# MLP of a hybrid encoder layer on one core: the first quarter of the hidden width takes the schedule of the next two

## The chip, the cores and the metric

One core of one Trainium2 chip runs the whole program as one launch. The metric is the device time of a run in microseconds (us). Three runs of the kernel before are given, and one execution was profiled.

## The reference, cut to what matters

One layer for 256 tokens of width 2048, all in float32: a mixer, a cross-attention, an MLP and a final norm. The change lies in the MLP and at the seam in front of it.

```python
    for l in range(DEPTH):
        ...
        x = x + cross_attention(h, mem_n, w_xq[l], w_xkv[l], w_xo[l])
        h = rms_norm(x, norm_ffn_g[l])
        x = x + jnp.square(jax.nn.relu(h @ w_ff1[l])) @ w_ff2[l]
    return rms_norm(x, norm_final_g)
```

`w_ff1` is 2048 x 8192, `w_ff2` is 8192 x 2048.

## The kernel before

**Precision.** Every matrix is split into a rounded part and the rest ("hi" and "lo", tiles `whi`/`wlo` for weights, the two halves of a `q` tile for activations). A product of two split matrices takes three matmuls, hi by hi, hi by lo and lo by hi. The weights come as float32 from memory, 1 MB a transfer, into one of three `raw` buffers. ScalarE writes hi (L125), VectorE writes lo (L126), in halves of 128x1024 each. There are three buffers for hi and three for lo, and from the MLP on every fourth half goes to a fourth pair, `whx`/`wlx` (`half_tiles`, L79), whose memory is free only once the attention's tiles have been read for the last time.

**The MLP.** The hidden width is worked in four quarters (`for fb in range(4)`, L1382). A quarter has two parts:

- First projection: eight blocks of 256 hidden features (`blocks`, L192 to L222). A block loads 2 MB of `w_ff1` and uses it in four pieces, each eight pairs of matmuls on TensorE (L210: 128x512, then 128x256). Its end is read by ScalarE and VectorE (L219, L220), squared after the ReLU (`evac_h`) and split again. I call the blocks of the first quarter A to H. In the order below, A writes `s_13017`/`s_13018`.
- Second projection: 512 hidden rows by 512 output columns is one block product per half of the tokens. `plain(n, q)` (L1232) computes one such block for both halves of the tokens, 24 matmuls of 128x512. Eight block products (two by two by two) can be had with seven products of sums of blocks (Strassen's form): `product` (L1254) is one of the seven, 12 matmuls; the sums of the weights are made by VectorE in place (L1261) between the products that need them, the sums of activations in `token_sums` (L1188). The four weight blocks of a unit lie in `b11`, `b12`, `b22`, `b21`, which are the tiles `rt` and `tr`, loaded by `load_block` (L1206, 1 MB each).

Quarters 1 to 3 compute two units in seven products. Their generator `with_seven` begins during the first projection, after the blocks D to H (`next(parts_of)`), and their matmuls are chained in one order (`ends`). The first quarter (the `else` branch, L1364 on) computes one unit with seven products and the rest plainly, all behind its first projection, and its matmuls are free to be put in another order by the scheduler.

**The residual.** The attention leaves the residual feature-major in `rt`. Four VectorE transposes (L1124) turn it into `tr`, and `place(b8)` (L1126) copies it from there token-major into `res`: 8 calls of 4 transfers, 64 KB each, in runs of 128 bytes. `tr` and `rt` are free for weight blocks when this is done. Before the transposes a TensorE product with ones (L1042) gives the norm's sums, and VectorE reads them (L1044).

**What sets the order.** Each engine works its instructions in the order in which the scheduler put them at build time. All transfers here are issued by one queue, SP's.

Of the kernel before, what the change touches and what calls it, by code (L numbers as in the profile page):

```python
# [52 lines left out]
def trunk(ctx: ExitStack, tc: tile.TileContext, x_f, mem_f, positions, lead_f, small_f, w_in, ret_gn_g, w_out, w_xq,  # L53
# [96 lines left out]
    def quad_a():  # L150
        return new_quad(hqp, 5)
# [1043 lines left out]
        vec.tensor_sub(sv[:, 3], a12, sv[:, 1])  # L1195
        split([a[:, i, :] for a in s_hl], sv.rearrange("p a s -> p (a s)"))

    def with_seven(hid, rows, last, early):

# [76 lines left out]
            own[n] = ps  # L1276
            opened.difference_update((n, t) for t in range(NT))

        if early:
            load_block(b11, 0, 0)  # L1280
            yield
            load_block(b12, 0, 1)
            product(shared, part(0, 0), b11, "shared", (b11, b12, b11))
            read((0, 0, shared))
            yield
            load_block(b22, 1, 1)
            product(p5, summed(0), b11, "p5", (b11, b22, b11))
            read((1, 0, p5), (1, 1, p5))
            yield
            load_block(b21, 1, 0)  # L1290
            product(shared, summed(1), b11, "shared", (b12, b22, b12))
            read((1, 0, shared))
            yield
            product(shared, summed(2), b12, "shared", (b11, b21, b11))
            read((0, 1, shared), (1, 1, shared))
            if last:
                product(p5, summed(3), b22, "p3")
                read((1, 0, p5))
            yield
            for n in range(2):  # L1300
                take(n, stream_ps())
            plain(0, 2)
            load_block(b12, 0, 3)
            if last:
                final.append(quad_a().both.rearrange("p k s -> p (k s)").bitcast(F32))
                with tc.issue_after(fetched[-1]):
                    nc.sync.dma_start(final[0], norm_final_g.partition_broadcast(P))
            if not last:
                product(own[1][0], summed(3), b22, (1, 0))
            plain(0, 3)  # L1310
            load_block(b22, 1, 3)
            product(own[0][0], part(1, 0), b21, (0, 0))
            read((0, 0, own[0][0], True))
            product(own[0][1], part(1, 1), b11, (0, 1))
            read((0, 1, own[0][1], True))
            plain(1, 2)
            load_block(b11, 0, 2)
            take(2, [bank(), bank()])
            plain(2, 2)
            load_block(b21, 1, 2)  # L1320
            opened.difference_update(("shared", "p5"))
            product(shared, part(0, 0), b11, "shared", (b11, b12, b11))
            read((2, 0, shared))
            plain(1, 3)
            read(*((1, t, own[1][t], True) for t in range(NT)))
            product(p5, summed(0), b11, "p5", (b11, b22, b11))
            read((3, 0, p5), (3, 1, p5))
            plain(2, 3)
            take(3, stream_ps())
            product(own[3][0], summed(3), b22, (3, 0), (b12, b22, b12))  # L1330
            plain(3, 2)
            product(shared, summed(1), b11, "shared", (b11, b21, b11))
            read((3, 0, shared))
            if not last:
                plain(3, 3)
                read(*((3, t, own[3][t]) for t in range(NT)))
                product(own[2][0], part(1, 0), b21, (2, 0))
                read((2, 0, own[2][0]))
                product(shared, summed(2), b12, "shared")
                read((2, 1, shared), (3, 1, shared))  # L1340
                product(own[2][1], part(1, 1), b11, (2, 1))
                read((2, 1, own[2][1]))
            else:
                product(own[2][0], part(1, 0), b21, (2, 0))
                read((2, 0, own[2][0], True), (2, 1, own[2][1]))
                plain(3, 3, True)
                of_7 = parted(b12)
                with tc.issue_after(latest["lo"]), tc.issue_after(latest["hi"]):
                    add(3, 0, own[3][0])
                    of_4 = parted(b11, quad_b)  # L1350
                with tc.high_priority(offset=50000):
                    settle(3, 0)
                    latest["lo"] = latest["add"]
                    mean_square(0)
                    r_0 = factor(0)
                    finish(0, r_0, (0, 512, act, nc.sync), (1024, 1536, act, nc.sync))
                for those in unscaled:
                    scale(*those)
                read((3, 1, own[3][1]))
                product(shared, summed(2), None, "shared", halves=of_7)  # L1360
                read((3, 1, shared, True), (2, 1, shared))
                ends_of = stream_ps()
                product(ends_of, part(1, 1), None, "end", halves=of_4)
                with tc.high_priority(offset=50000):  # L1364
                    with tc.issue_after(latest["square"]):
                        finish(0, r_0, (512, 1024, act, nc.sync), (1536, D, act, nc.sync))
                    junk = fp.tile([P, 2, S], F32, name="hs", tag="hs", bufs=2)
                    for c, ps in enumerate(ends_of):
                        with tc.issue_after(latest["lo"]):
                            got = add(2, 1, ps[:, :256], c * 256, c * 256 + 256)  # L1370
                        acc = ssq4[:, 1, 3 + c:4 + c]
                        vec.scalar_tensor_tensor(junk[:, c], got, 1.0, got, op0=ALU.mult, op1=ALU.mult, accum_out=acc)
                        if c:
                            vec.scalar_tensor_tensor(sums[1], acc, 1.0 / D, sums[1], op0=ALU.mult, op1=ALU.add)
                        else:
                            mean_square(1)
                    finish(1, factor(1), (0, 256, act, nc.sync), (512, 1024, vec, act), (256, 512, act, nc.sync),
                           (1024, 1536, vec, nc.sync), (1536, D, vec, act))
        else:
            for n in range(2):  # L1380
                take(n, stream_ps())
            own[2] = own[3] = [bank(), bank()]  # L1382
            plain(3, 0)
            load_block(b11, 0, 0)
            plain(3, 1)
            load_block(b12, 0, 1)
            product(shared, part(0, 0), b11, "shared", (b11, b12, b11))
            read((0, 0, shared))
            plain(3, 2)
            load_block(b22, 1, 1)  # L1390
            product(p5, summed(0), b11, "p5", (b11, b22, b11))
            read((1, 0, p5), (1, 1, p5))
            plain(0, 2)
            product(own[1][0], summed(3), b22, (1, 0), (b12, b22, b12))
            plain(3, 3)
            load_block(b21, 1, 0)
            read(*((3, t, own[3][t]) for t in range(NT)))
            product(shared, summed(1), b11, "shared", (b11, b21, b11))
            read((1, 0, shared))
            plain(0, 3)  # L1400
            product(own[0][0], part(1, 0), b21, (0, 0))
            read((0, 0, own[0][0]))
            plain(2, 0)
            plain(1, 2)
            product(shared, summed(2), b12, "shared")
            read((0, 1, shared), (1, 1, shared))
            plain(2, 1)
            product(own[0][1], part(1, 1), b11, (0, 1))
            read((0, 1, own[0][1]))
            plain(2, 2)  # L1410
            plain(2, 3)
            read(*((2, t, own[2][t]) for t in range(NT)))
            plain(1, 3)
# [5 lines left out]
    for fb in range(4):  # L1419
        hid = []  # L1420
        rows = w_ff2[0, fb * D:(fb + 1) * D, :]
        early = fb > 0
        parts_of = with_seven(hid, rows, fb == 3, early)
        ends.clear()
        for b2 in range(8):
            hs = fp.tile([P, 2, S], F32, name="hs", tag="hs", bufs=2)
# [1 line left out]
                hid.append(quad_a())  # L1428

            def evac_h(b, ps):  # L1430
                if early:
                    act.activation(ps, ps, AF.Relu)
                    act.activation(hs[:, b, :], ps, AF.Square)
                else:
# [12 lines left out]
        for _ in parts_of:  # L1447
            pass

# [41 lines left out]
```

## Time and profile before

| | |
|---|---|
| runs | 2045.98 us median of 3 (2044.49 to 2046.55) |
| span of the profiled execution, first to last instruction | 2043.3 us |
| the profiled execution's own time | not given apart; the median of the runs is 2.7 us above its span |
| busy share of the span | TensorE 99%, weight loads 86%, VectorE 76%, ScalarE 58%, GpSimd 2% |
| granted TensorE clock, mean | 0.998 |
| moved by DMA | 405.24 MB, mean 198 GB/s |

The busy shares are means over all stages; what a stage is worth has to be read from the stage itself. A busy TensorE is one with a matmul in flight. The pace of the matmuls is read from the distance of their starts, which is less than the duration of one since they overlap.

### The profile page before, as it was taken

How to read it: one execution, taken by the hardware profiler on the slowest of the kernel's cores; microseconds unless marked ns; L12 is line 12 of the kernel's file. 1: busy time of each engine (PE TensorE's matmuls, PEld its weight loads, DVE VectorE, ACT ScalarE, POOL GpSimd, SP SyncE). 2: the span in 40 equal slices, each digit the busy share in tenths (PEclk: the TensorE clock that was granted, in tenths of full speed). 3: DMA queues.
4: the chain of work that ended last, by engine and by line, in shares of the span. 5: the costliest groups of instructions: out<-in, count | busy, mean ns of one | idle time of the engine just before them, and what ended most of it. 6: DMA issues, size and time to landing. Idle time of an engine off the chain costs nothing.

```text
span 2043.3 us, 28453 instructions
## 1 busy us (share of the span) xinstructions
PE 2030.5 (99%) x10802; PEld 1751.4 (86%) x10802; DVE 1550.6 (76%) x2423; ACT 1184.3 (58%) x1941; POOL 38.7 (2%) x50
## 2 busy tenths in 40 slices
PE   9999999999999999999999999999999999999998
PEld 7888888988888888888888899888888888888886
DVE  5887788779667875888567666777867887888788
ACT  6655764575457554755446565555547656656655
POOL 0000000000000000000000000000000000000000
PEclk9999999999999999999999999999999999999999
DMA  9689556466555655555467655569657656665761
GB/s 329 209 259 303 184 185 197 154 189 201 180 166 183 198 190 165 186 181 190 156 212 244 191 183 163 174 180 254 221 168 234 219 163 214 201 204 166 242 231 62
DMA packets 329370, 405.24 MB, mean 198 GB/s; under 512 B 34944, under 2 KB 239632, under 8 KB 329104
## 3 DMA queue, kind: packets, MB, share of 16 engines
q1 hardware_dynamic: 328800, 402.74, 62.2%
q8 instruction: 84, 1.38, 0.3%
q10 hardware_dynamic: 432, 0.69, 0.1%
q14 instruction: 54, 0.44, 0.1%
HBM read 389.74 MB, written 11.55 MB: 196 GB/s over the span
## 4 chain that ended last, share of the span: by engine, by line
PE 97%; DVE 2%; issue 0%; DMA 0%; ACT 0%; SPq 0%; DVEq 0%; POOLq 0%; POOL 0%; ACTq 0%
PE s L210 52%; PE s L167 8%; PE s L168 8%; PE s L166 8%; PE b L1227 7%; PE s L1227 7%; PE s L400 1%; PE s L401 1%; PE s L402 1%; PE b L795 1%; PE b L698 1%; PE b L138 1%; PE b L828 1%; PE b L137 1%; PE b L139 1%
## 5 line engine op out<-in xcount | busy, mean ns | idle before, releaser
L210 PE MATMUL s<-q,whi 128*128 128x512 f32 x2816 | 969.0, 390 | 0.6 <-DVE bo L220 0.6
L126 DVE TENSOR_TENSOR wlo<-raw,whi 128x1024 fp32r<-128x1024 f32 x586 | 715.1, 1222 | 296.3 <-ACT whi L125 291.7
L125 ACT ACTIVATE whi<-raw 128x1024 fp32r<-128x1024 f32 x586 | 620.8, 1060 | 488.9 <-PE s L210 209.2
L210 PE MATMUL s<-q,wlo 128*128 128x256 f32 x2816 | 765.0, 281 | 0.0
L210 PEld LDWEIGHTS s<-q,whi 128*128 128x128 f32 x2816 | 520.6, 188 | 101.4 <-DVE bo L220 0.9
L210 PEld LDWEIGHTS s<-q,wlo 128*128 128x128 f32 x2816 | 527.2, 188 | 12.6 <-DVE wlo L126 0.5
L167 PE MATMUL s<-wlo,q 128*128 128x512 f32 x704 | 277.2, 394 | 0.0
L168 PE MATMUL s<-whi,q 128*128 128x512 f32 x704 | 274.9, 391 | 0.0
L166 PE MATMUL s<-whi,q 128*128 128x512 f32 x704 | 254.4, 391 | 0.0
L166 PEld LDWEIGHTS s<-whi,q 128*128 128x128 f32 x704 | 132.1, 188 | 27.4
L168 PEld LDWEIGHTS s<-whi,q 128*128 128x128 f32 x704 | 132.3, 188 | 26.2
L167 PEld LDWEIGHTS s<-wlo,q 128*128 128x128 f32 x704 | 132.3, 188 | 26.2
L219 ACT ACTIVATE bo<-s 128x256 f32<-128x256 f32 x192 | 73.2, 381 | 105.5 <-PE s L210 105.5
L220 DVE TENSOR_TENSOR bo<-bo,s 128x256 f32<-128x256 f32 x192 | 79.9, 416 | 43.0 <-ACT bo L219 42.8
L1227 PE MATMUL s<-whi,q 128*128 128x512 f32 x280 | 90.4, 389 | 0.0
L1250 DVE TENSOR_TENSOR wlo<-rt,whi 128x1024 fp32r<-128x1024 f32 x54 | 65.8, 1224 | 32.3 <-ACT whi L1249 31.6
L210 PE MATMUL s<-q,whx 128*128 128x512 f32 x256 | 89.2, 389 | 0.0
L125 ACT ACTIVATE whx<-raw 128x1024 fp32r<-128x1024 f32 x58 | 61.5, 1060 | 43.2 <-PE b L1227 17.2
L126 DVE TENSOR_TENSOR wlx<-raw,whx 128x1024 fp32r<-128x1024 f32 x58 | 70.9, 1222 | 17.9 <-ACT whx L125 17.4
L1249 ACT ACTIVATE whi<-rt 128x1024 fp32r<-128x1024 f32 x54 | 57.2, 1060 | 38.1 <-PE s L1227 17.8
L210 PE MATMUL s<-q,wlx 128*128 128x256 f32 x256 | 70.4, 280 | 0.0
L1227 PE MATMUL b<-whi,q 128*128 128x512 f32 x216 | 70.3, 389 | 0.0
(350 smaller groups left out, 2372.2 us busy)
## 6 DMA issues: line engine op xcount, KB each, us to landing
raw<-w_in SPq DMA_DIRECT2D x143, 1024.0 KB
raw<-w_ff SPq DMA_DIRECT2D x100, 1024.0 KB
raw<-w_xkv SPq DMA_DIRECT2D x29, 1024.0 KB
raw<-w_out SPq DMA_DIRECT2D x16, 1024.0 KB
raw<-w_xq SPq DMA_DIRECT2D x16, 1024.0 KB
raw<-w_xo SPq DMA_DIRECT2D x16, 1024.0 KB
rt<-w_ff SPq DMA_DIRECT2D x14, 1024.0 KB
tr<-w_ff SPq DMA_DIRECT2D x14, 1024.0 KB
```

Source lines behind the costliest of these rows:

```text
L125: latest["hi"] = act.activation(hi[:, cs], src[:, cs], AF.Copy).ins
L126: latest["lo"] = vec.tensor_sub(lo[:, cs], src[:, cs], hi[:, cs].bitcast(F32)).ins
L137: pe.matmul(o, lhs[0], rhs[0], start=first, stop=False)
L166: pe.matmul(o, xh, wh, start=first, stop=False)
L167: pe.matmul(o, xh, wl, start=False, stop=False)
L168: pe.matmul(o, xl, wh, start=False, stop=last)
L210: ins = pe.matmul(ps[b][:, :S] if part else ps[b], halves[h][part][:, i, b * P:(b + 1) * P], x[:, kk % 4, :], start=kk == 0 and not part, ...
L219: act.activation(o, ps[b][:, S:], AF.Copy)
L220: vec.tensor_add(o, o, ps[b][:, :S])
L1227: ins = pe.matmul(o, lhs[l], rhs[r], start=key not in opened, stop=last and j == 2, skip_group_check=True).ins
L1249: latest["hi"] = act.activation(hi, raw[:, c:c + 1024], AF.Copy).ins
L1250: latest["lo"] = vec.tensor_sub(lo, raw[:, c:c + 1024], hi.bitcast(F32)).ins
```

## The change

The `else` branch of `with_seven` is gone. The first quarter runs the same code as quarters 1 and 2: two units in seven products, the generator begun after block D, ReLU and square by ScalarE instead of one VectorE instruction, the matmuls of the projection chained in `ends`. So that `rt` and `tr` are free in time, the calls of `place` move forward: one to two after each of the blocks A to F instead of one after each of A to H.

```diff
-    def with_seven(hid, rows, last, early):
+    def with_seven(hid, rows, last):
...
-        if early:
...
-        else:
-            for n in range(2):
-                take(n, stream_ps())
-            own[2] = own[3] = [bank(), bank()]
-            plain(3, 0)
-            load_block(b11, 0, 0)
-            plain(3, 1)
-            load_block(b12, 0, 1)
-            product(shared, part(0, 0), b11, "shared", (b11, b12, b11))
-            read((0, 0, shared))
-            plain(3, 2)
...
-            plain(2, 2)
-            plain(2, 3)
-            read(*((2, t, own[2][t]) for t in range(NT)))
-            plain(1, 3)
-            read(*((1, t, own[1][t]) for t in range(NT)))
...
             def evac_h(b, ps):
-                if early:
-                    act.activation(ps, ps, AF.Relu)
-                    act.activation(hs[:, b, :], ps, AF.Square)
-                else:
-                    vec.scalar_tensor_tensor(hs[:, b, :], ps, 0.0, ps, op0=ALU.max, op1=ALU.mult)
+                act.activation(ps, ps, AF.Relu)
+                act.activation(hs[:, b, :], ps, AF.Square)
...
-            blocks(h3, w_ff1[0], fb * D + b2 * 256, 2, evac_h, ends if early else None)
-            if early and b2 > 2:
+            blocks(h3, w_ff1[0], fb * D + b2 * 256, 2, evac_h, ends)
+            if fb == 0:
+                for b8 in ((0,), (1, 2), (3,), (4, 5), (6,), (7,), (), ())[b2]:
+                    place(b8)
+            if b2 > 2:
                 next(parts_of)
-            if fb == 0:
-                place(b2)
```

What this does to the order of the instructions is shown at three places. Quarters 1 to 3 keep their order on all engines; only the names of the fourth pair of weight buffers fall on other halves.

First, TensorE at the seam, from the end of block A's third piece. Before:

```order
L210 MATMUL s_13018<-q,whi 128x512
L210 MATMUL s_13018<-q,wlo 128x256
L210 MATMUL s_13127<-q,whi 128x512
L210 MATMUL s_13127<-q,wlo 128x256
L210 MATMUL s_13128<-q,whi 128x512
L210 MATMUL s_13128<-q,wlo 128x256
L210 MATMUL s_13127<-q,whi 128x512
L210 MATMUL s_13127<-q,wlo 128x256
L1042 MATMUL b<-ones,acc_12125 128x2 x2
L210 MATMUL s_13128<-q,whi 128x512
```

Here `s_13127` and `s_13128` are block B. Before, B's pieces go on behind these rows, with the first two `whx` matmuls of block A in their midst. After the change, from the same point:

```order
L210 MATMUL s_13018<-q,whi 128x512
L210 MATMUL s_13018<-q,wlo 128x256
L1042 MATMUL b<-ones,acc_12125 128x2 x2
L210 MATMUL s_13017<-q,whx 128x512
L210 MATMUL s_13018<-q,whx 128x512
L210 MATMUL s_13017<-q,wlx 128x256
L210 MATMUL s_13018<-q,wlx 128x256
```

The product with ones moves forward by three pairs, and block A's last piece (`whx`, `wlx`) follows at once. Block B begins only behind it.

Second, VectorE at the same place. Before:

```order
L126 TENSOR_TENSOR wlo<-raw,whi 128x1024 x2
L1044 TENSOR_SCALAR n_s<-b 128x2
L1124 STREAM_TRANSPOSE tr<-rt 128x1024 x4
L126 TENSOR_TENSOR wlx<-raw,whx 128x1024
L1115 TENSOR_TENSOR rstd3q<-n_r 128x2
L126 TENSOR_TENSOR wlo<-raw,whi 128x1024 x2
```

After:

```order
L126 TENSOR_TENSOR wlo<-raw,whi 128x1024
L1044 TENSOR_SCALAR n_s<-b 128x2
L1124 STREAM_TRANSPOSE tr<-rt 128x1024 x4
L126 TENSOR_TENSOR wlo<-raw,whi 128x1024
L1115 TENSOR_TENSOR rstd3q<-n_r 128x2
L126 TENSOR_TENSOR wlx<-raw,whx 128x1024
```

The lo of block B's third piece, before the transposes until now, stands behind them, and ahead of `wlx`, the lo of block A's last piece.

Third, SP's queue from the fifth load of `w_ff1` on (`raw`: half of a block's weights, 1 MB; `res`: a transfer of `place`; `rt`, `tr`: `load_block`). Before:

```order
L113 DMA raw<-w_ff 128x8x256 x5
L1131 DMA res<-tr 32x16x32 x2
L113 DMA raw<-w_ff 128x8x256
L1131 DMA res<-tr 32x16x32 x3
L113 DMA raw<-w_ff 128x8x256
L1131 DMA res<-tr 32x16x32 x4
L113 DMA raw<-w_ff 128x8x256
L1131 DMA res<-tr 32x16x32 x7
L113 DMA raw<-w_ff 128x8x256 x2
L1131 DMA res<-tr 32x16x32 x4
```

After:

```order
L113 DMA raw<-w_ff 128x8x256 x5
L1131 DMA res<-tr 32x16x32 x4
L113 DMA raw<-w_ff 128x8x256
L1131 DMA res<-tr 32x16x32 x10
L113 DMA raw<-w_ff 128x8x256
L1131 DMA res<-tr 32x16x32 x2
L113 DMA raw<-w_ff 128x8x256
L1210 DMA rt<-w_ff 128x4x512
L1131 DMA res<-tr 32x16x32 x7
L113 DMA raw<-w_ff 128x8x256
L1131 DMA res<-tr 32x16x32
L113 DMA raw<-w_ff 128x8x256
```

Ahead of the first load of block E (the ninth `raw`) stand 23 transfers of `place` and one weight block, where there were 16 transfers of `place`.

## Rows read from the trace of the kernel before

**Rows 1.** The page, part 1: busy time, share of the span, instructions.

```profile
PE 2030.5 (99%) x10802; PEld 1751.4 (86%) x10802; DVE 1550.6 (76%) x2423; ACT 1184.3 (58%) x1941; POOL 38.7 (2%) x50
```

**Rows 2.** TensorE's waits: for whom, us in total, times, longest.

```profile
PE s L210 <- DVE bo L220: 0.6, 1, 0.6
```

**Rows 3.** Stretches: us, busy us (instructions) by engine, clock, DMA share, GB/s.

```profile
1335.00:1340.00 5.00, 5.00 (x31) 4.45 (x30) 3.73 (x6) 2.88 (x6) 0.00 (x0) 1.00 0.62 193
1368.00:1457.00 89.00, 88.42 (x485) 76.60 (x483) 67.13 (x106) 47.29 (x70) 0.00 (x0) 1.00 0.96 267
1425.00:1430.00 5.00, 5.00 (x31) 4.38 (x30) 3.55 (x6) 2.62 (x5) 0.00 (x0) 1.00 1.05 392
1540.00:1700.00 160.00, 160.00 (x816) 136.78 (x815) 131.98 (x153) 96.97 (x133) 0.00 (x0) 1.00 0.60 196
```

**Rows 4.** Timeline of TensorE, second projection: start, us, engine, line, operation.

```profile
1460.17 0.62 PE L1227 MATMUL s<-whi,q 128*128 128x512 f32 x2
...
1462.89 0.39 PE L1227 MATMUL s<-whx,q 128*128 128x512 f32 x1
```

**Rows 5.** Timeline of TensorE at the seam; in brackets idle time and releaser.

```profile
1357.14 0.39 PE L210 MATMUL s<-q,whi 128*128 128x512 f32 x1
...
1357.48 0.50 PE L1042 MATMUL b<-ones,acc 128*128 128x2 f32 x4
1357.84 0.47 PE L210 MATMUL s<-q,whi 128*128 128x512 f32 x1
...
1362.38 0.63 PE L210 MATMUL s<-q,whx 128*128 128x512 f32 x2
...
1367.93 0.28 PE L210 MATMUL s<-q,wlx 128*128 128x256 f32 x1
1368.79 0.50 PE L210 MATMUL s<-q,whi 128*128 128x512 f32 x1 [0.58 <-DVE bo L220]
```

**Rows 6.** Timeline of VectorE at the seam.

```profile
1355.19 1.23 DVE L126 TENSOR_TENSOR wlo<-raw,whi 128x1024 fp32r<-128x1024 f32 x1 [1.08 <-ACT whi L125]
...
1358.82 0.15 DVE L1044 TENSOR_SCALAR n_s<-b 128x2 f32<-128x2 f32 x1
1358.88 4.61 DVE L1124 STREAM_TRANSPOSE tr<-rt 128x1024 f32<-128x1024 f32 x4
1363.42 1.18 DVE L126 TENSOR_TENSOR wlx<-raw,whx 128x1024 fp32r<-128x1024 f32 x1
1364.52 0.15 DVE L1115 TENSOR_TENSOR rstd3q<-n_r 128x2 f32<-128x2 f32 x1
1364.59 2.35 DVE L126 TENSOR_TENSOR wlo<-raw,whi 128x1024 fp32r<-128x1024 f32 x2
1368.31 0.42 DVE L220 TENSOR_TENSOR bo<-bo,s 128x256 f32<-128x256 f32 x1 [1.37 <-ACT bo L219]
```

**Rows 7.** Timeline of ScalarE: at the seam, and block E's first load.

```profile
1356.58 1.06 ACT L125 ACTIVATE whi<-raw 128x1024 fp32r<-128x1024 f32 x1 [1.43 <-PE s L210]
1358.02 1.06 ACT L125 ACTIVATE whx<-raw 128x1024 fp32r<-128x1024 f32 x1 [0.38 <-PE b L1042]
...
1391.75 1.06 ACT L125 ACTIVATE whi<-raw 128x1024 fp32r<-128x1024 f32 x1 [4.14 <-DMA raw<-w_ff]
```

**Rows 8.** The clock behind the last matmuls: a stretch, columns as in rows 3.

```profile
2034.00:2036.00 2.00, 0.00 (x0) 0.00 (x0) 1.72 (x7) 1.86 (x4) 0.00 (x0) 0.82 0.49 182
```

**Rows 9.** Timeline of TensorE: its last matmuls.

```profile
2030.30 3.03 PE L1227 MATMUL s<-q 128*128 128x256 f32 x24
```

**Rows 10.** Timeline of SP's queue: issues of transfers.

```profile
1386.32 7.05 SPq L1131 DMA_DIRECT2D res<-tr  x4
...
1414.56 6.90 SPq L1131 DMA_DIRECT2D res<-tr  x4
```

**Rows 11.** The page, part 5: the lo of weights on VectorE; mean ns behind the busy time.

```profile
L126 DVE TENSOR_TENSOR wlo<-raw,whi 128x1024 fp32r<-128x1024 f32 x586 | 715.1, 1222 | 296.3 <-ACT whi L125 291.7
```

**Rows 12.** Line L1261 on VectorE, sums of weight blocks: duration in ns, min/median/max.

```profile
L1261 DVE TENSOR_TENSOR rt<-tr,rt x42: 1215/1218/1220, 1454.9 to 2015.9; 128x1024 f32<-128x1024 f32 x42
```

More of the change, by code (lines that the diff above doesn't have):

```diff
@@ new lines, in with_seven @@
+        load_block(b11, 0, 0)
+        yield
+        load_block(b12, 0, 1)
+        product(shared, part(0, 0), b11, "shared", (b11, b12, b11))
+        read((0, 0, shared))
+        yield
+        load_block(b22, 1, 1)
+        product(p5, summed(0), b11, "p5", (b11, b22, b11))
+        read((1, 0, p5), (1, 1, p5))
+        yield
+        load_block(b21, 1, 0)
+        product(shared, summed(1), b11, "shared", (b12, b22, b12))
+        read((1, 0, shared))
+        yield
+        product(shared, summed(2), b12, "shared", (b11, b21, b11))
@@ new lines, in with_seven @@
+        read((0, 1, shared), (1, 1, shared))
+        if last:
+            product(p5, summed(3), b22, "p3")
+            read((1, 0, p5))
+        yield
+        for n in range(2):
+            take(n, stream_ps())
+        plain(0, 2)
+        load_block(b12, 0, 3)
+        if last:
+            final.append(quad_a().both.rearrange("p k s -> p (k s)").bitcast(F32))
+            with tc.issue_after(fetched[-1]):
+                nc.sync.dma_start(final[0], norm_final_g.partition_broadcast(P))
@@ new lines, in with_seven @@
+        if not last:
+            product(own[1][0], summed(3), b22, (1, 0))
+        plain(0, 3)
+        load_block(b22, 1, 3)
+        product(own[0][0], part(1, 0), b21, (0, 0))
+        read((0, 0, own[0][0], True))
+        product(own[0][1], part(1, 1), b11, (0, 1))
+        read((0, 1, own[0][1], True))
+        plain(1, 2)
+        load_block(b11, 0, 2)
+        take(2, [bank(), bank()])
+        plain(2, 2)
+        load_block(b21, 1, 2)
+        opened.difference_update(("shared", "p5"))
@@ new lines, in with_seven @@
+        product(shared, part(0, 0), b11, "shared", (b11, b12, b11))
+        read((2, 0, shared))
+        plain(1, 3)
+        read(*((1, t, own[1][t], True) for t in range(NT)))
+        product(p5, summed(0), b11, "p5", (b11, b22, b11))
+        read((3, 0, p5), (3, 1, p5))
+        plain(2, 3)
+        take(3, stream_ps())
+        product(own[3][0], summed(3), b22, (3, 0), (b12, b22, b12))
+        plain(3, 2)
+        product(shared, summed(1), b11, "shared", (b11, b21, b11))
+        read((3, 0, shared))
@@ new lines, in with_seven @@
+        if not last:
+            plain(3, 3)
+            read(*((3, t, own[3][t]) for t in range(NT)))
+            product(own[2][0], part(1, 0), b21, (2, 0))
+            read((2, 0, own[2][0]))
+            product(shared, summed(2), b12, "shared")
+            read((2, 1, shared), (3, 1, shared))
+            product(own[2][1], part(1, 1), b11, (2, 1))
+            read((2, 1, own[2][1]))
+        else:
+            product(own[2][0], part(1, 0), b21, (2, 0))
+            read((2, 0, own[2][0], True), (2, 1, own[2][1]))
+            plain(3, 3, True)
+            of_7 = parted(b12)
+            with tc.issue_after(latest["lo"]), tc.issue_after(latest["hi"]):
+                add(3, 0, own[3][0])
+                of_4 = parted(b11, quad_b)
+            with tc.high_priority(offset=50000):
+                settle(3, 0)
+                latest["lo"] = latest["add"]
+                mean_square(0)
+                r_0 = factor(0)
+                finish(0, r_0, (0, 512, act, nc.sync), (1024, 1536, act, nc.sync))
+            for those in unscaled:
+                scale(*those)
+            read((3, 1, own[3][1]))
+            product(shared, summed(2), None, "shared", halves=of_7)
+            read((3, 1, shared, True), (2, 1, shared))
+            ends_of = stream_ps()
+            product(ends_of, part(1, 1), None, "end", halves=of_4)
+            with tc.high_priority(offset=50000):
+                with tc.issue_after(latest["square"]):
+                    finish(0, r_0, (512, 1024, act, nc.sync), (1536, D, act, nc.sync))
+                junk = fp.tile([P, 2, S], F32, name="hs", tag="hs", bufs=2)
+                for c, ps in enumerate(ends_of):
+                    with tc.issue_after(latest["lo"]):
+                        got = add(2, 1, ps[:, :256], c * 256, c * 256 + 256)
+                    acc = ssq4[:, 1, 3 + c:4 + c]
+                    vec.scalar_tensor_tensor(junk[:, c], got, 1.0, got, op0=ALU.mult, op1=ALU.mult, accum_out=acc)
+                    if c:
+                        vec.scalar_tensor_tensor(sums[1], acc, 1.0 / D, sums[1], op0=ALU.mult, op1=ALU.add)
+                    else:
+                        mean_square(1)
+                finish(1, factor(1), (0, 256, act, nc.sync), (512, 1024, vec, act), (256, 512, act, nc.sync),
+                       (1024, 1536, vec, nc.sync), (1536, D, vec, act))
@@ L1421, in trunk @@
         rows = w_ff2[0, fb * D:(fb + 1) * D, :]
-        early = fb > 0
-        parts_of = with_seven(hid, rows, fb == 3, early)
+        parts_of = with_seven(hid, rows, fb == 3)
         ends.clear()
```

118 lines of the change are left out of this document (removed).

## The prediction

> **What bounds the kernel now.** I read the page's busy times first [rows 1]: TensorE is busy in 99% of the span, so a change pays only if TensorE gets fewer matmuls or has fewer gaps. Then TensorE's waits [rows 2]: in the whole MLP it waits once, 0.6 us, at the seam between the attention's last projection and the first quarter [rows 5]. In a stretch of quarter 1, which has the schedule that the first quarter is to get, it is busy in 160 of 160 us at full clock, with VectorE at 132 and ScalarE at 97 [rows 3]. So the matmuls that go are worth their pace, and a new gap costs its length. The rest is read at the seam, from the timelines of TensorE, VectorE and ScalarE [rows 5 to 7], and for the transfers from the stretches [rows 3] and SP's queue [rows 10].
>
> **The matmuls that go.** Before, the first quarter has 12 plain blocks of 24 matmuls and 7 products of 12: 372. After, 8 and 14: 360. Twelve matmuls started between 1460.17 and 1462.89 [rows 4], 2.72 us or 0.227 each (the 0.39 in the row is a duration, and they overlap). The twelve that go are worth **2.72 us**.
>
> **What VectorE and ScalarE get.** Two more products than plain blocks taken out, at two halves each: 3 x 2 = 6 more splits (14 products and 8 plain blocks are 22 units of 1 MB, against 19), 1.22 us each on VectorE [rows 11]; 8 more sums of weight blocks at 1.22 [rows 12]; six more adds into the residual; against that, 16 ReLU instructions leave for ScalarE. The splits and sums are 14 x 1.22 = 17 us more on VectorE, and the adds and the ReLUs about balance. I cost it at nothing: quarter 1 carries the same load, and TensorE doesn't wait there [rows 3]. Without that cover, each late half would cost up to 1.22.
>
> **The seam.** Here the change moves two things, and a chain that was hidden comes to light. Before, TensorE did the product with ones at 1357.48, worked on with block B, came to A's last piece (`whx`) at 1362.38 only and to `wlx` after that [rows 5]. In that shelter VectorE read the norm's sums at 1358.82, transposed for 4.54 us (start to next start) and wrote `wlx` from 1363.42 [rows 6]. After, A's last piece follows the product with ones at once, and `wlx` stands behind the transposes and one more half. In steps:
>
> - Three pairs at 0.34 (1357.14 to 1357.48) now stand behind the product with ones instead of ahead: it starts at 1356.46. It takes TensorE 0.36 (to 1357.84), until 1356.82. Its result released ScalarE 0.54 after its start (1358.02 [rows 7]), so it is there at 1357.00.
> - ScalarE writes block B's third hi from 1356.58 for 1.06 [rows 7], then `whx`, until 1358.70. TensorE follows a release by 0.06 (VectorE's read of 1368.31 ends at 1368.73, TensorE starts at 1368.79 [rows 5, 6]): `whx` starts at 1358.76, a gap of **1.94**. Two `whx` matmuls take 0.45, to 1359.21.
> - VectorE is free from 1356.42 [rows 6]. Norm sums at 1357.00, transposes from 1357.06 to 1361.60, the lo of B's third piece 1.10 to 1362.70, L1115 0.07, `wlx` from 1362.77 for 1.18, to 1363.95 [rows 6]. TensorE goes on at 1364.01: a second gap of **4.80**.
> - What falls away is the old wait for a bank at 1368.79: after the matmul of 1367.93 the next was due at 1368.05, so **0.74** [rows 5].
>
> Net at full clock: +1.94 + 4.80 - 0.74 - 2.72 = **+3.3 us**.
>
> **The clock.** At the end of the program the last 24 matmuls start at 2030.30 and are through at 2033.33 [rows 9]; in the stretch from 2034 to 2036 the granted clock has a mean of 0.82 [rows 8], which is 0.64 of it at full and 0.36 at half clock, so it fell from 2.4 to 1.2 GHz at 2035.28, 2.0 us after the last matmul. Nothing in the two gaps (6.7 us with 0.45 of work between) keeps it up, so I take it that TensorE goes on at half clock at 1364. No row shows how soon it comes back under load. Bounds: no loss (back at once), and a low stretch as long as the second gap, 4.8, which loses half of it, 2.4. I take a low stretch of 3.4, midway between the 2.0 that the fall took and 4.8: **+1.7 us**, an estimate.
>
> The Trainium skill ("TensorE: Matmul & The Clock Gate", section "Why this matters for your kernels") warns of idle gaps of more than some three microseconds between bursts of matmuls, after which the engine is back at its lower clock; this speaks against the change. By that rule the first gap alone would do nothing and the second would lower the clock, and the sum stays above +3.3; by row 8 alone, which shows a fall with no work behind it, the sum could be +3.3. The trace agrees on the fall, at 2.0 us, earlier than the page has it, and no row of this kernel shows the return.
>
> **The transfers.** From 1368 to 1457 the DMA engines are taken to 0.96 [rows 3], so what is put ahead of a load delays it. In 1335 to 1340 they moved 193 GB/s at 0.62, so 1 MB of `w_ff1` takes 3.37 us of them all; in 1425 to 1430 392 GB/s, so 1 MB of a weight block takes 2.68 [rows 3]. Three rounds of four `place` transfers and two loads took from 1386.32 to 1414.56 [rows 10], 9.41 each, so a transfer of `place` takes (9.41 - 6.74) / 4 = 0.67. Before, block E's first load was there at 1391.75 [rows 7], just in time. Now 7 transfers and one weight block more stand ahead of it, 4.7 + 2.7, and the queue starts 1.9 earlier (transposes through at 1361.6, not 1363.5): there at 1397.3. TensorE comes to block E at 1364.01 + 14 x 0.172 + 3 x 11.0 = 1399.4, plus the loss by the clock, and needs the load 2.1 before (hi and lo): 1397.3 to 1399.0. So it is just in time again, by less than 2 us: I cost it at nothing. If SP's issue pace of 7.05 for four [rows 10] were the true price of a transfer, 1.76, the load would come 7.6 us later than that and cost up to 7.6; the stretches' price is nearer, since those 7.05 us hold the two loads ahead of them too.
>
> **Sum.** -2.72 + 1.94 + 4.80 - 0.74 + 1.7 = +5.0 us: the span of 2043.3 becomes 2048.3, and with the 2.7 us that lie between it and the median of the runs **2051.0 us**, against 2045.98. About 0.2%, 4.1 us, is what a measurement of this kernel can tell from no change: same is 2041.9 to 2050.1.
>
> **Rivals.**
>
> - **A, the clock costs nothing.** It comes back at once, or does not fall. For: 0.45 us of matmuls lie between the gaps, and no row shows a return. Against: the fall after 2.0 us. Time: 2045.98 + 3.3 = 2049.3, within 0.2%.
> - **B, the loads come late.** The forward move of `place` makes block E or F wait as well, on top of the forecast. For: no margin was left before, and E's first load is the ninth behind a busy DMA. Against: the gap at the seam gives the queue time. With 2 to 4 us of stall: 2053 to 2055.
> - **C, the other side: the seam stays covered.** Place: VectorE between the norm's sums and `wlx`. If the chain of transposes and lo is there when TensorE needs it, what is left is -2.72 - 0.74 = -3.5, or 2042.5. It decides at a total gap of 3.5: below that the change isn't slower. For: before, TensorE never waited here. Against: the order puts 4.54 + 1.10 + 1.18 us of VectorE between the norm's sums and `wlx`, and TensorE has 0.45 us of work for it.
>
> **How the numbers follow.** Forecast 0.56, A 0.20, B 0.14, C 0.10. The forecast lies above 2050.1 if the clock costs more than 0.8 of its 0 to 2.4: 0.44 slower, 0.12 same. A gives 0.18 same, 0.02 slower, B 0.14 slower, C 0.05 same and 0.05 faster, as the runs spread by 2 us. So slower 0.60, same 0.35, faster 0.05. The range leaves out C and the upper half of B; it goes from A with a gap 1.5 us shorter and runs 1 us low, 2046.8, to 2054.5.
>
> **What would show it.** Right: TensorE idle before the first `whx` by about 1.9 us, released by ScalarE, and before the first `wlx` by about 4.8, released by VectorE's L126; the granted clock below 1.00 only in the stretch around 1359 to 1370; twelve matmuls of L1227 fewer; no wait at E to H; quarters 1 to 3 as long as before. Wrong: `wlx` before the transposes in VectorE's timeline, no idle time at L1042, or waits of ScalarE for `raw` that reach TensorE at blocks D to F (then B).

## The result and the profile after

| | before | after |
|---|---|---|
| runs, us | 2045.41 median of 6 (2044.49 to 2046.55) | 2050.96 median of 6 (2049.62 to 2052.51) |
| ratio | | 1.0028, 95% interval 1.0017 to 1.0039 |
| span of the profiled execution, us | 2043.3 | 2050.8 (a run of 2052.51) |
| granted TensorE clock, mean | 0.998 | 0.996 |

The change is slower by 5.55 us, 0.27%. Forecast were 2051.0 us and +5.0.

The page, part 1, of the kernel after, against [rows 1]:

```profile
PE 2032.2 (99%) x10790; PEld 1753.2 (85%) x10790; DVE 1563.7 (76%) x2427; ACT 1202.1 (59%) x1979; POOL 39.8 (2%) x50
```

TensorE has the twelve matmuls fewer (10802 to 10790), VectorE 13.1 us and ScalarE 17.9 us more to do. The waits of TensorE in the kernel after (for whom: us in total, times, longest) against [rows 2]:

```profile
PE s L210 <- DVE wlx L126: 4.7, 1, 4.7
PE s L210 <- ACT whx L125: 1.7, 1, 1.7
```

The old wait for a bank is gone and two new ones stand in its place. From 1372 to 2025 TensorE does not wait at all; the sum over the stretches of that time (TensorE is busy in 653 of 653 us):

```profile
sum 653.00, PE 653.00 PEld 559.64 DVE 533.23 ACT 400.42 POOL 0.00; mean PE 108.83 PEld 93.27 DVE 88.87 ACT 66.74 POOL 0.00
```

The timeline of TensorE at the seam of the kernel after, against [rows 5]; in brackets the idle time and who ended it:

```profile
1358.52 0.50 PE L1042 MATMUL b<-ones,acc 128*128 128x2 f32 x4
1360.70 0.73 PE L210 MATMUL s<-q,whx 128*128 128x512 f32 x2 [1.69 <-ACT whx L125]
1366.12 0.80 PE L210 MATMUL s<-q,wlx 128*128 128x256 f32 x2 [4.68 <-DVE wlx L126]
1366.71 0.63 PE L210 MATMUL s<-q,whx 128*128 128x512 f32 x1
...
1367.35 0.63 PE L210 MATMUL s<-q,whx 128*128 128x512 f32 x1
...
1404.10 0.28 PE L210 MATMUL s<-q,wlx 128*128 128x256 f32 x1
1404.22 0.39 PE L210 MATMUL s<-q,whi 128*128 128x512 f32 x1
...
2037.79 3.03 PE L1227 MATMUL s<-q 128*128 128x256 f32 x24
```

Behind the second gap a pair takes 0.64 us (1366.71 to 1367.35) instead of 0.344. The stretches of the kernel after (columns as in [rows 3]; the clock stands behind the busy times) show when:

```profile
1360.00:1361.00 1.00, 0.29 (x1) 0.30 (x2) 1.00 (x2) 0.65 (x1) 0.00 (x0) 1.00 0.79 175
1361.00:1362.00 1.00, 0.44 (x2) 0.00 (x1) 1.00 (x2) 0.00 (x0) 0.00 (x0) 0.79 0.84 236
1362.00:1370.00 8.00, 3.88 (x13) 3.41 (x14) 4.06 (x5) 0.00 (x0) 0.00 (x0) 0.50 0.65 143
1370.00:1372.00 2.00, 2.00 (x8) 1.71 (x8) 0.75 (x2) 1.81 (x4) 0.00 (x0) 0.54 0.98 304
1372.00:1404.00 32.00, 32.00 (x187) 28.35 (x187) 19.09 (x34) 19.07 (x34) 0.00 (x0) 1.00 0.95 218
```

The second of them, with a mean clock of 0.79, is 0.58 of that microsecond at 2.4 GHz and 0.42 at 1.2: the clock fell at 1361.58. A mean of 0.54 over 1370 to 1372 puts its return at 1371.84 by the same working; the pairs are at full pace from 1371.83. TensorE worked at half clock from 1366.12 on, for 5.7 us. Why `wlx` is late is read from VectorE's timeline of the kernel after, against [rows 6]:

```profile
1359.06 0.16 DVE L1044 TENSOR_SCALAR n_s<-b 128x2 f32<-128x2 f32 x1 [0.57 <-PE b L1042]
1359.13 4.61 DVE L1124 STREAM_TRANSPOSE tr<-rt 128x1024 f32<-128x1024 f32 x4
1363.67 1.18 DVE L126 TENSOR_TENSOR wlo<-raw,whi 128x1024 fp32r<-128x1024 f32 x1
1364.77 0.15 DVE L1115 TENSOR_TENSOR rstd3q<-n_r 128x2 f32<-128x2 f32 x1
1364.84 1.22 DVE L126 TENSOR_TENSOR wlx<-raw,whx 128x1024 fp32r<-128x1024 f32 x1
```

The norm's sums, the transposes, one more half and only then `wlx`, which was next to the transposes before. ScalarE's timeline of the kernel after has `whx` and block E's first load, against [rows 7]:

```profile
1358.65 1.06 ACT L125 ACTIVATE whi<-raw 128x1024 fp32r<-128x1024 f32 x1 [1.43 <-PE s L210]
1359.61 1.04 ACT L125 ACTIVATE whx<-raw 128x1024 fp32r<-128x1024 f32 x1
...
1401.21 1.06 ACT L125 ACTIVATE whi<-raw 128x1024 fp32r<-128x1024 f32 x1 [5.34 <-DMA raw<-w_ff]
```

E's load was there at 1401.21, 3.0 us ahead of E's first matmul at 1404.22, which needs 2.1 of it for hi and lo.

**The account.** Ahead of the seam the programs are alike, but one execution reaches it up to 2 us later than another. (Half of these 2 us arise in the first 10 us of the program: there the change's matmul pairs of L400 to L402 start 0.43 apart in this execution and 0.33 in that of before.) So I count from the end of A's third piece (1356.46 before, 1358.52 after: the start of the product with ones where that follows at once, 1.02 before it where three pairs lie between) to the start of the last 24 matmuls. Before that is 2030.30 - 1356.46 = 673.84, after 2037.79 - 1358.52 = 679.27: **+5.43**. It falls into two parts at the second matmul pair of block E (1394.34 and 1404.57). Behind it 635.96 before, 633.22 after: -2.74, which is the twelve matmuls and nothing else. Ahead of it +8.17. In that lie the first gap, 1360.70 - 1358.88 = 1.82; the second, 1366.12 - 1361.15 = 4.97; the old wait, -0.74; and the clock, which the fourth run below measures as 2.62. They make 8.67. Of the 0.5 too much, 0.16 is a late lo in E that the kernel before had; 0.3 I did not trace.

### The profile page after: what moved, and what is told of

Read it like the earlier page. It is cut to its first block, busy times and chain, and to the rows that moved or that the text cites. A ratio compares the mean times of both kernels' runs of the same rounds, so it can differ in the third digit from the quotient of the medians.

```text
span 2050.8 us, 28473 instructions
## 1 busy us (share of the span) xinstructions
PE 2032.2 (99%) x10790; PEld 1753.2 (85%) x10790; DVE 1563.7 (76%) x2427; ACT 1202.1 (59%) x1979; POOL 39.8 (2%) x50
## 4 chain that ended last, share of the span: by engine, by line
PE 96%; DVE 2%; DMA 1%; issue 0%; ACT 0%; SPq 0%; DVEq 0%; POOLq 0%; POOL 0%; ACTq 0%
PE s L210 51%; PE s L167 8%; PE s L168 8%; PE s L166 8%; PE s L1227 7%; PE b L1227 7%; PE s L400 1%; PE s L401 1%; PE s L402 1%; PE b L795 1%; PE b L698 1%; PE b L138 1%; PE b L828 1%; PE b L137 1%; PE b L139 1%
## 5 line engine op out<-in xcount | busy, mean ns | idle before, releaser
L126 DVE TENSOR_TENSOR wlo<-raw,whi 128x1024 fp32r<-128x1024 f32 x598 | 729.1, 1221 | 285.1 <-ACT whi L125 280.5
L125 ACT ACTIVATE whi<-raw 128x1024 fp32r<-128x1024 f32 x598 | 633.8, 1060 | 498.2 <-PE s L210 213.7
L167 PE MATMUL s<-wlo,q 128*128 128x512 f32 x704 | 277.2, 394 | 0.0
L168 PE MATMUL s<-whi,q 128*128 128x512 f32 x704 | 274.9, 391 | 0.0
L166 PE MATMUL s<-whi,q 128*128 128x512 f32 x704 | 254.4, 391 | 0.0
L166 PEld LDWEIGHTS s<-whi,q 128*128 128x128 f32 x704 | 132.1, 188 | 27.3
L168 PEld LDWEIGHTS s<-whi,q 128*128 128x128 f32 x704 | 132.3, 188 | 26.3
L1227 PE MATMUL s<-whi,q 128*128 128x512 f32 x384 | 122.1, 389 | 0.0
L1227 PEld LDWEIGHTS s<-whi,q 128*128 128x128 f32 x384 | 72.1, 188 | 14.9
L1227 PE MATMUL s<-wlo,q 128*128 128x512 f32 x192 | 74.7, 389 | 0.0
```

The source lines that it names most:

```text
L125: latest["hi"] = act.activation(hi[:, cs], src[:, cs], AF.Copy).ins
L126: latest["lo"] = vec.tensor_sub(lo[:, cs], src[:, cs], hi[:, cs].bitcast(F32)).ins
L166: pe.matmul(o, xh, wh, start=first, stop=False)
L167: pe.matmul(o, xh, wl, start=False, stop=False)
L168: pe.matmul(o, xl, wh, start=False, stop=last)
L1227: ins = pe.matmul(o, lhs[l], rhs[r], start=key not in opened, stop=last and j == 2, skip_group_check=True).ins
```

## The experiments

My theory is that of the prediction: the chain of the pieces uncovers VectorE's work between the norm's sums and `wlx`, and the clock falls in the gap. The rivals were A (the clock costs nothing), B (the transfers) and C (the seam stays covered, or could be). In the table the median of each kernel, that of the kernel before among the same runs, the ratio's interval, and the stretch from the seam to the last 24 matmuls in the profiled execution against 673.84.

| run | median, us | before, us | 95% interval of the ratio | seam to end, us |
|---|---|---|---|---|
| the change | 2050.96 | 2045.41 | 1.0017 to 1.0039 | +5.43 |
| 1 chain_only | 2053.47 | 2044.88 | 1.0026 to 1.0053 | +9.91 |
| 2 free_two | 2053.79 | 2044.88 | 1.0032 to 1.0057 | +8.83 |
| 3 late_turn | 2049.95 | 2044.88 | 1.0015 to 1.0034 | +6.34 |
| 4 filler | 2050.02 | 2044.88 | 1.0014 to 1.0033 | +4.81 |
| 5 places_only | 2048.93 | 2045.25 | 1.0007 to 1.0025 | +2.55 |
| 6 free_two_shift | 2051.05 | 2045.25 | 1.0018 to 1.0039 | +6.72 |
| 7 free_two_pool | 2054.76 | 2045.25 | 1.0038 to 1.0063 | +8.71 |
| 8 shift_between | 2044.56 | 2045.10 | 0.9990 to 1.0008 | -2.23 |
| 9 shift_between2 | 2045.07 | 2045.10 | 0.9990 to 1.0009 | -1.05 |

**1. The chain alone, in the kernel before.**

```diff
-    ends = []
+    ends, chain = [], []
...
-            blocks(h3, w_ff1[0], fb * D + b2 * 256, 2, evac_h, ends if early else None)
+            blocks(h3, w_ff1[0], fb * D + b2 * 256, 2, evac_h, ends if early else chain)
```

> The kernel before with one edit: the pieces of the first quarter's first projection keep their written order (the chain of ends that quarters 1 to 3 have); the first quarter's products and the transfers stay as before. The prediction's seam says that this chain alone opens the gaps: TensorE idle before the first whx by about 1.7 to 1.9 us and before the first wlx by about 4.7 to 4.8, the old wait for a bank gone, all 372 matmuls of the quarter kept. With the clock's cost as the changed kernel's trace shows it (2.6 us): -0.74 + 6.8 + 2.6 = +8.7, 2054 us against 2045.4. With a clock that costs nothing: +6.0, 2051.5. A rival, by which the gaps come of the seven-product schedule or of the earlier transfers and not of the chain: no gap at the seam, 2045.4.

The waits of TensorE in this run, columns as above:

```profile
PE s L210 <- DVE wlx L126: 4.7, 1, 4.7
PE s L210 <- ACT whx L125: 1.7, 1, 1.7
```

The two gaps of the change, to a tenth, with none of its products and with the calls of `place` where they were: the chain makes them. (The scheduler does let some small transfers out earlier here, twelve instead of five ahead of block D's first load, but no wait of TensorE is for a load.) The cost is +8.6 by the medians, against +8.7 expected; the rival without a gap is out. The profiled execution, the slowest of the five, has +9.9. The 1.2 on top is no wait: its matmul pairs start 0.353 apart from 1371 to 1449, where those of the change start 0.344 apart; why is open. The change, with twelve matmuls fewer, is 2.5 us below this run (3.0 when each is taken against the kernel before among its own runs), where 2.7 were due.

**2. The change without the chain for blocks A and B.**

```diff
-            blocks(h3, w_ff1[0], fb * D + b2 * 256, 2, evac_h, ends)
+            blocks(h3, w_ff1[0], fb * D + b2 * 256, 2, evac_h, ends if fb or b2 > 1 else None)
```

> The changed kernel without the chain for the first two blocks of the first quarter's projection, A and B; all else as in the change. By the prediction's steps the seam is covered again by block B, both gaps and the clock's loss go, and what is left is the twelve matmuls: 2045.4 - 2.7 = 2042.7, or 2042.0 if the old wait for a bank goes too. The rival is the transfers: without the gaps TensorE comes to block E about 9 us earlier than in the changed kernel, while the same nine or so transfers stand ahead of E's first load, which in the changed kernel was converted at 1401.2 just ahead of its use at 1404.2. Then TensorE waits at E for about 5 to 7 us and the time is 2046 to 2049.

The gaps at the seam are gone, yet nothing is won: +8.9 by the medians. The waits of TensorE in this run:

```profile
PE s L210 <- ACT whi L125: 4.2, 2, 3.9
PE s L210 <- DVE wlo L126: 3.4, 3, 2.2
PE s L210 <- DVE bo L220: 0.6, 1, 0.6
```

The timelines of this run: ScalarE's read of E's first load, and the issues of SP's queue ahead of it:

```profile
1398.11 1.06 ACT L125 ACTIVATE whi<-raw 128x1024 fp32r<-128x1024 f32 x1 [6.60 <-DMA raw<-w_ff]
...
1377.74 1.08 SPq L113 DMA_DIRECT2D raw<-w_ff  x1
1378.86 0.58 SPq L1210 DMA_DIRECT2D rt<-w_ff  x1
1379.48 11.14 SPq L1131 DMA_DIRECT2D res<-tr  x6
1390.73 0.56 SPq L113 DMA_DIRECT2D raw<-w_ff  x1
```

Between D's second load and E's first stand a weight block of 1 MB (`rt`) and six small transfers. TensorE waits 3.91 us for E (1395.31 to 1399.22), and the clock falls there too, as the stretches of this run show:

```profile
1398.00:1399.00 1.00, 0.00 (x0) 0.00 (x0) 0.00 (x0) 0.89 (x1) 0.00 (x0) 1.00 0.91 125
1399.00:1400.00 1.00, 0.59 (x1) 0.19 (x1) 0.80 (x1) 1.00 (x3) 0.00 (x0) 0.74 0.98 164
1400.00:1406.00 6.00, 5.52 (x18) 4.75 (x19) 2.16 (x3) 1.45 (x2) 0.00 (x0) 0.50 0.99 311
```

So rival B, which the change itself does not show, is what the seam's gaps hid: with the clock they gave the queue some 8 us more up to block E. It came out worse than I had put it (2046 to 2049), as I had left out the clock and a later wait at G (2.24).

**3. The transposes behind block A's last weights, with the chain.**

```diff
-    for c in range(4):
-        vec.transpose(...)
...
+            if fb == 0 and b2 == 0:
+                with tc.issue_after(latest["lo"]):
+                    for c in range(4):
+                        vec.transpose(...)
```

> The changed kernel with VectorE's four transposes moved from ahead of to behind block A's last weights (wlo, wlx); the chain of the pieces stays. By the prediction's seam the second gap is the transposes standing ahead of wlx: it shrinks from 4.7 us to 1 at most, the first stays near 1.7, and the clock stays at full speed or falls for less than 2 us. Time: before -2.7 -0.7 +1.8 +0.8 = 2044.5. If the second gap has another cause (a weight load that comes late), it stays at 4 or more: 2050 to 2051. The transfers into the residual begin some 3 us later, and if the prediction's rival B holds, TensorE waits for a load at E or F by 2 to 5 us: 2047 to 2050.

TensorE's timeline of this run at the seam:

```profile
1359.46 0.73 PE L210 MATMUL s<-q,whx 128*128 128x512 f32 x2 [1.69 <-ACT whx L125]
1360.98 0.50 PE L210 MATMUL s<-q,wlx 128*128 128x256 f32 x2 [0.79 <-DVE wlx L126]
```

The second gap goes from 4.7 to 0.8: it was the transposes. The other waits are for loads, 1.0 us at E's second, 1.5 at F's first and 1.5 at G's first, within the 2 to 5 us of rival B, and the medians give +5.1. The clock's part I had wrong: I expected it to hold, or to be low for less than 2 us. The stretches of this run:

```profile
1360.00:1361.00 1.00, 0.21 (x2) 0.02 (x1) 1.00 (x2) 0.00 (x0) 0.00 (x0) 1.00 0.90 278
1361.00:1362.00 1.00, 1.00 (x5) 0.90 (x6) 1.00 (x1) 0.00 (x0) 0.00 (x0) 0.74 1.05 370
1363.00:1364.00 1.00, 1.00 (x5) 0.90 (x4) 1.00 (x2) 0.00 (x0) 0.00 (x0) 0.50 0.86 239
1364.00:1365.00 1.00, 1.00 (x5) 0.81 (x5) 1.00 (x2) 0.37 (x1) 0.00 (x0) 0.56 0.95 315
```

It fell at 1361.5, when TensorE was at work again, and came back at 1364.9. Gaps of 1.69 and 0.79 us with 0.45 of matmuls between were enough.

**4. Work in place of the idle time.** 28 matmuls more, whose result nothing uses, between the product with ones and `whx`.

```diff
+                if filler and g == h == 1:
+                    with tc.issue_after(ends[-1]):
+                        for i in range(28):
+                            ins = pe.matmul(filler[0], quads[i % 4].both[:, 0, :P], quads[0].both[:, 1, :], start=True, stop=True).ins
+                    ends.append(ins)
...
+    idle = bank()
...
-            blocks(h3, w_ff1[0], fb * D + b2 * 256, 2, evac_h, ends)
+            blocks(h3, w_ff1[0], fb * D + b2 * 256, 2, evac_h, ends, filler=None if fb or b2 else [idle])
```

> The changed kernel with 28 matmuls (128x512, about 6.4 us in all) into a spare bank put between the product with ones and the first whx, whose result nothing uses. They add no wait for block A's weights: wlx still comes when VectorE has written it, and the gaps are filled up with work instead of idle time. If the low clock costs 2.6 us behind the gaps, as the pace of its pairs in the changed kernel says (0.64 against 0.344 over 5.6 us), the granted clock stays at 1.00 here and the time is 2051.0 - 2.6 = 2048.4. If the clock costs nothing (rival A), or the low pace behind the gaps has another cause, the time stays at 2051.0.

TensorE's timeline of this run:

```profile
1357.89 6.64 PE L209 MATMUL b<-q 128*128 128x512 f32 x28
1364.38 0.63 PE L215 MATMUL s<-q,whx 128*128 128x512 f32 x2
1365.13 0.50 PE L215 MATMUL s<-q,wlx 128*128 128x256 f32 x2
...
1400.49 0.28 PE L215 MATMUL s<-q,wlx 128*128 128x256 f32 x1
1400.97 0.50 PE L215 MATMUL s<-q,whi 128*128 128x512 f32 x1 [0.20 <-ACT whi L125]
1402.23 0.38 PE L215 MATMUL s<-q,wlo 128*128 128x256 f32 x1 [0.76 <-DVE wlo L126]
```

The granted clock is 1.00 in every stretch from 1355 to 1376; two of them, at and behind the place of the second gap:

```profile
1364.00:1366.00 2.00, 1.88 (x10) 1.31 (x9) 1.07 (x1) 0.00 (x0) 0.00 (x0) 1.00 0.68 88
1366.00:1368.00 2.00, 2.00 (x13) 1.77 (x13) 0.19 (x1) 0.61 (x2) 0.00 (x0) 1.00 0.77 122
```

The same work, from the first `wlx` to the last of block D, takes 35.36 us here (1365.13 to 1400.49) and 37.98 in the change (1366.12 to 1404.10): **the clock costs 2.62 us**, and rival A is out. The time of the whole run does not show it: 2050.0, not 2048.4, and its interval holds the change's ratio. In the profiled execution 1.4 of the 2.6 go again at E, where TensorE, that much earlier, now waits for the load (1400.60 to 1400.97, and 1401.20 to 1402.23).

**5. The transfers alone moved forward, in the kernel before.**

```diff
-            if fb == 0:
-                place(b2)
+            if fb == 0:
+                for b8 in ((0,), (1, 2), (3,), (4, 5), (6,), (7,), (), ())[b2]:
+                    place(b8)
```

> The kernel before with one edit: the transfers into the residual in the change's order (one, two, one, two, one, one of eight groups behind blocks A to F instead of one behind each of A to H); its products and its unchained pieces stay as before. On the queue 9 of the small transfers stand between the loads of blocks D and E instead of 7, then 5 and 5 instead of 4. By the prediction's price of a small transfer (0.67 us) E's load, which was just in time before, comes 1.3 us later and F's 2 us: TensorE waits 1 to 2 us in all, about 2046.5. By the queue's pace (1.76 us each, the prediction's other bound) it waits 3.5 us or more: 2048.5 or later. If the forward move costs nothing, 2044.9.

The timelines of TensorE and of ScalarE in this run:

```profile
1357.17 0.50 PE L1042 MATMUL b<-ones,acc 128*128 128x2 f32 x4
...
1392.92 1.06 ACT L125 ACTIVATE whi<-raw 128x1024 fp32r<-128x1024 f32 x1 [5.45 <-DMA raw<-w_ff]
```

E's load comes 35.75 us after the product with ones, against 1391.75 - 1357.48 = 34.27 before [rows 5, 7]: 1.48 us for two small transfers, 0.74 each. The waits, at E's two loads and F's first, are 2.1 us, the profiled execution has +2.55, the medians +3.7 (interval 1.4 to 5.1). The forward move costs something. The load's lateness in the trace is near the lower of the two prices; with SP's pace of 1.76 it would have been 3.5. The time is not: the median of 2048.9 is above the 2046.5 that I had put for the lower price and within what I had put for the higher. The profiled execution, at 2047.3, is among the faster of eleven that lie between 2046.7 and 2050.3, and no trace shows what the slower ones wait for.

**6. As run 2, and the seven-product schedule begun one block later.**

```diff
-                for b8 in ((0,), (1, 2), (3,), (4, 5), (6,), (7,), (), ())[b2]:
+                for b8 in ((0,), (1,), (2,), (3,), (4,), (5,), (6, 7), ())[b2]:
...
-            if b2 > 2:
+            if b2 > 2 + (fb == 0):
```

> The run without the chain for blocks A and B, and the seven-product schedule of the first quarter begins one block later: its first block of the second weight is loaded behind block E's first load instead of ahead of it, and the groups of transfers stand one behind each block up to F, two behind G. The cause named for the run without the chain is that E's first load came 6.3 us later than in the kernel before, with one load of 1 MB more ahead of it. If so, E's load is back at its place of before, TensorE waits neither at the seam nor at E, the clock stays at full, and what is left is 2044.9 - 2.7 - 0.7 = 2041.5, or up to 2 us more if the loads of F to H come late for the same reason. If the transfers' sum is what is too large, whatever their order, waits of 4 us or more stay and the time is 2047 or later.

TensorE's waits in this run:

```profile
PE b L1227 <- DVE res L1142: 4.7, 1, 4.7
PE s L210 <- DVE wlo L126: 1.4, 2, 1.0
```

E's load is back (34.6 us after the product with ones, 34.3 before), as expected. But a wait that neither theory named takes its place. The fourth and the fifth product write the same bank, and in this order nothing stands between them: TensorE stopped at 1447.9 and waited until 1452.66 for VectorE's read, which stood behind sums and splits in VectorE's queue. The clock fell there too (0.50 from 1452 to 1458), and with that the time is 2051.05 where I had put 2041.5 to 2043.5.

**7. As run 2, with the residual's transfers on GpSimd's queue.**

```diff
-                nc.sync.dma_start(to, tr[32 * a:32 * a + 32, :, b8 * 32:b8 * 32 + 32])
+                nc.gpsimd.dma_start(to, tr[32 * a:32 * a + 32, :, b8 * 32:b8 * 32 + 32])
```

> The run without the chain for blocks A and B, with the transfers into the residual issued from GpSimd's queue instead of SP's; their number, order and bytes stay. If the weights' loads are late because they stand behind the small transfers on one queue, they now pass them, E's load is in time, and the time is 2041.5 to 2043. If the DMA engines themselves are full (share 0.81 to 1.05 between 1372 and 1436 in the run on SP's queue), the two queues share them and the waits of about 7 us stay or move: 2048 to 2054.

The timeline of TensorE in this run at block E:

```profile
1403.46 0.79 PE L210 MATMUL s<-q,whi 128*128 128x512 f32 x1 [8.37 <-ACT whi L125]
```

Its stretch ahead of that wait:

```profile
1384.00:1395.00 11.00, 10.77 (x62) 9.09 (x60) 6.26 (x12) 4.94 (x10) 6.84 (x11) 1.00 1.07 255
```

E's load is later still (read by ScalarE at 1402.35, in run 2 at 1398.11), although SP issued it at 1378.94, and in run 2 at 1390.73. So its place in SP's queue is not what holds it. The DMA engines' share is 1.07 to 1.09 from 1372 to 1410, which points to full engines; this run does not isolate them, since the small transfers also change their form (1024 packets in all from GpSimd's queue, 16384 of less than 512 bytes from SP's). The Trainium skill ("DMA: Bandwidth & Descriptors", section "Issuing engines are not separate DMA queues") says that DMAs started by several engines end on the same DMA engines; this trace agrees, as the load issued earlier came later.

**8 and 9. As run 6, with a plain block between the two products; then the transfers spread once more.**

```diff
-        product(shared, summed(2), b12, "shared", (b11, b21, b11))
-        read((0, 1, shared), (1, 1, shared))
+        if not first:
+            product(shared, summed(2), b12, "shared", (b11, b21, b11))
+            read((0, 1, shared), (1, 1, shared))
...
         plain(0, 2)
+        if first:
+            product(shared, summed(2), b12, "shared", (b11, b21, b11))
+            read((0, 1, shared), (1, 1, shared))
```

> The run whose schedule begins one block later, with one more edit: the first plain block of the second weight (24 matmuls) stands between the fourth and the fifth product, which share a bank; without it the fifth waited 4.7 us for VectorE's read of the fourth, at 1452, and ran 12 matmuls at the low clock behind that. If that wait and the clock behind it are the rest of the loss, the 4.7 and the some 2.5 of the clock go, what is left of the waits is the 2.0 at the seam and at the loads of E and H, and the time is 2051.0 - 7 = 2044 (2043.9 from the other side: 2045.2 - 2.7 + 1.4 of waits that the kernel before hasn't). If a further wait follows in its place, it stays at 2047 or more.

Run 9 has one line more:

```diff
-                for b8 in ((0,), (1,), (2,), (3,), (4,), (5,), (6, 7), ())[b2]:
+                for b8 in ((0,), (1,), (2,), (3,), (4,), (5, 6), (7,), ())[b2]:
```

> The same with the groups of transfers one behind each of blocks A to E, two behind F, one behind G instead of two behind G, so that 4 instead of 8 small ones stand between two of the weights' loads there. If H's load (1.0 us late in the run before it) was late by those eight, that wait goes: 2043. If it moves to G, no change against the run beside it.

TensorE's waits in run 8:

```profile
PE s L210 <- DVE bo L220: 0.6, 1, 0.6
PE s L210 <- DVE wlo L126: 0.6, 1, 0.6
```

One of the two is the old wait for a bank, the other H's load. From the seam to the end it is 2.23 us shorter than before: 2.72 less by the matmuls, 0.5 more by H. In the medians that is 0.5 us and cannot be told from none. (In the profiled executions 1.3 of the 2.2 are lost as well: in the first 10 us, where the two programs are alike, run 8's falls that much behind that of before.) But run 8 is 6.5 us below run 6, about the 7 expected. Run 9 has a wait of 0.5 at G beside that at H: the load's lateness moved and did not go.

## Why the prediction was right

- **The matmuls that go** (2.72): right. 2.74 behind block E, and 2.5 to 3.0 between run 1 and the change.
- **What VectorE and ScalarE get** (nothing): right. TensorE is busy in 653.0 of the 653 us from 1372 to 2025.
- **The seam** (+1.94, +4.80, -0.74): right in each step, measured +1.82, +4.97, -0.74. The whole of it is 0.05 off. Run 1 shows the chain as the cause of both gaps, run 3 the transposes as that of the second.
- **The clock** (+1.7): the mechanism was right and the size too small; 2.62 was measured, above the upper end of 2.4 that I had given it. I had taken the low stretch under load as between nothing and the length of the gap, 4.8. It was 5.7. The length of the gap was no bound for how long the clock stayed down behind it. The rule of the Trainium skill that I weighed against row 8 ("TensorE: Matmul & The Clock Gate", section "Why this matters for your kernels": no idle gaps of more than some three microseconds) would have left the clock alone in run 3, whose gaps are 1.69 and 0.79; that trace does not agree, and it decides.
- **The transfers** (just in time): right by 0.9 us (3.0 ahead of E, 2.1 needed). From the product with ones the load took 42.7 us (1401.21 - 1358.52), where 40.8 were forecast (1397.3 - 1356.46), and E itself came 1.0 later by the clock, so that of a margin of 1.7 there were 0.9 left; had the clock cost what I had put, the load would have been just at the edge. It was right also for the reason given against rival B, the gap at the seam. A small transfer was priced 0.67 and measured 0.74, in one execution of run 5. What I had not seen is how much this ties the terms together: gaps and clock were not only a loss, they were what the queue lived on.
- **The sum** (+5.0, 2051.0): +5.55 by the medians, +5.43 from the seam to the end. That the time forecast meets the median of 2050.96 to 0.04 is luck: the three runs that the forecast started from have a median 0.57 above that of the six (2045.98 against 2045.41), and this hides that the difference was put 0.55 too low. Of the 0.92 that the clock's term lacked, 0.5 do not show in the total: 0.16 is the late lo that the kernel before had at E, the rest was not traced (the account above).
- **Rivals.** A is refuted by run 4. B is not in the change, but is what stands behind it (runs 2, 3 and 7). C, "if the seam is covered, 2042.5", was wrong as I worked it out, though it did not come: covering the seam alone gives 2053.8, since B then takes its place. Runs 6 and 8 show what more it takes, and the -3.5 shrink to -2.2 in one execution, -0.5 in the medians.

## What to carry to other kernels

Before taking out a gap, ask what the gap feeds: here the idle 7 us at the seam and the low clock behind it gave the busy DMA engines (a share of 0.95 from 1372 to 1404) their time, and each run that removed or shortened them alone met the next limit, first a load, then a bank. Writing one fixed order for pieces that the scheduler had interleaved costs what it uncovers, and the price can be read ahead from the other engine's queue between the release and the late tile. Short gaps close together can cost the clock as a long one does: in run 3 those of 1.69 and 0.79 us brought it down, and a single one of 2.24 in run 2 did not. What decides between the two these runs do not show.

## What had not been expected of the hardware

- In run 3 the clock fell 0.5 us after TensorE had gone back to work, behind gaps of 1.69 and 0.79; in run 2 it fell at 1399.5, 0.3 us after the end of a gap of 3.91, and then held 0.50 for six microseconds of waiting work. But the gap of 2.24 in run 2, at 1434.88, left it at 1.00 throughout (1430 to 1438).
- With TensorE at work the return took 5.7 us in the change and 3.9 in run 3 (1360.98 to 1364.9).
- SP issued six small transfers in 11.14 us in run 2, with the DMA engines at a share of 0.87, and four in 2.75 in the change (from 1363.82), with a share of 0.39: the pace at which a queue issues is not the price of a transfer.
